# Seven-product f tiles from tile 1 on, first-half products first, and sums of h inside the norm chain

## The chip, the cores and the metric

The kernel runs on one core of a Trainium2 chip. The metric is the device time of one execution in microseconds. The engines are TensorE (PE, with its weight loads as PEld), VectorE (DVE), ScalarE (ACT), GpSimd (POOL) and SyncE (SP), which issues the transfers. Each engine works through its own queue in order and waits on semaphores for the others.

## The reference, cut to what matters

Two layers; each is a half-step SwiGLU feed-forward block, a token mixer (a 2-D Fourier transform in layer 0, neighbourhood attention in layer 1) and a second feed-forward block. Every one of these six sublayers has a norm ahead of it and one behind it, with scales and shifts that come from a modulation vector.

```python
def _modulation(cond, w_mod, b_mod):
    m = jax.nn.silu(cond) @ w_mod + b_mod
    return m.reshape(cond.shape[0], N_MOD, D_MODEL)

def _modulated_prenorm(x, g, m, k):
    return _rmsnorm(x, g) * (1 + m[:, 3 * k + 1, None]) + m[:, 3 * k, None]

def _swiglu(h, w1, w2):
    gate, up = jnp.split(h @ w1, 2, axis=-1)
    return (jax.nn.silu(gate) * up) @ w2

def _half_ffn(x, m, k, g_pre, g_post, w1, w2):
    h = _modulated_prenorm(x, g_pre, m, k)
    return x + 0.5 * m[:, 3 * k + 2, None] * _rmsnorm(_swiglu(h, w1, w2), g_post)
```

There are 640 tokens (512 latent, 128 context), D_MODEL is 1024 and D_FF 2816. All inputs are float32.

## The kernel before, in words

Data lies transposed: channels on the 128 partitions, tokens along the free dimension. A model width of 1024 is 8 chunks of 128, D_FF is 22 tiles of 128 ("f tiles"), and the 640 tokens are two halves of 320 columns. The sublayers are numbered n = 0 to 5; 0, 2, 3 and 5 are feed-forward, 1 is the Fourier mixer, 4 the attention.

**Precision.** Each operand is split in two parts, hi (ACT rounds it, L191 for weights and L202 for data) and lo (DVE subtracts hi, L193 and L203), and each product of a 128 x 128 weight block with 320 columns is three matmuls, hi by hi, hi by lo and lo by hi (`mm3`, L208 to L210). POOL takes the lo of six weight units at the start, DVE all others.

**Weights** arrive as units of 128 x 1024 (512 KB) in the pool `raw` of 4 buffers, and their hi and lo go to the pool `wts` of 6 pairs or, for some, to blocks of the ring of 20 blocks that also holds h, the hidden values and the stream x. `unit(i)` sends, that is loads and splits, up to three units ahead of the one that is asked for (`send`, L165).

**A feed-forward layer** (`ffn`, L514) multiplies h by w1 (gate and up, L517 on), applies silu(gate) * up, and multiplies the hidden tile by w2. Plain f tiles take 8 block products, each of 4 chunks by one half: gate and up, two halves of the chunks, two halves of the tokens. Fast f tiles (`w1_fast`, L586) take seven by a Strassen scheme: with gate and up as one factor, the first and second four chunks, and the two token halves, 2 x 2 blocks are multiplied with seven products of sums. For these, sums of the weights are formed on DVE as the unit is sent (L176 to L178, L184), sums of h are formed on DVE between the plain tiles of the second half (`combine`, L576, split at L203), and DVE adds the products up (L600 to L619). Before, tiles 4 to 19 are fast and 0 to 3, 20 and 21 plain. The plan (`plan_ffn`) runs tiles 0 and 1, 2, 3 for the first half of the tokens, the same for the second half with the steps of `combine` between them, then the fast tiles, and last 20 and 21. After tiles 4, 8, 12 and 16 it runs the w2 products of the slice before (8 output chunks by two halves), and at the end those of the last slice, one half after the other.

**Modulation.** The modulation vectors of later sublayers are formed beside the feed-forward layers: 128 products of a 128 x 1024 unit with the condition rows, two DVE instructions each (`gemv`, L348). BEHIND gives how many units a layer takes (28, 20, 28, 28, 24, 0); the calls of `w2` of the first four slices release them evenly (7 units a slice for 28). Their loads use the pool `raw` too.

**Norm chains.** At a layer's end and for each half a chain is launched (`boundary`): the post-norm of the layer, the addition to x, and the pre-norm of the next (`post`, `pre`). Its steps are woven into the stream of matmuls by a clock of estimated time (`tick`). Its two groups of small matmuls (L423 for the sums of squares, L431 to spread the result) are put behind the latest matmul in PE's queue at the place where the step runs. `pre` then scales y by the norm (L455), applies scale and shift (L461 on DVE for odd chunks, L463 on ACT for even), and splits the result into h (L202, L203). x is spilled to memory during the layer, to make room, and loaded back.

## Time and profile before

| what | value |
|---|---|
| time, median of 3 runs | 2402.0 us (2401.56 to 2404.12) |
| the profiled execution, its own time | 2403.8 us |
| its span, first to last instruction | 2402.0 us |
| mean granted clock of TensorE in it | 0.992 |
| PE busy | 2339.2 us, 15692 matmuls |
| DVE busy | 1740.3 us, 3112 instructions |
| ACT busy | 1275.4 us, 2436 instructions |
| DMA, read from memory | 263 MB, 114 GB/s over the span |

A row of the timeline has the start in us, the duration, the engine, the line of the code, the operation with what it writes and reads, the shape, a count of neighbours that were put together, and in brackets the idle time of the engine just ahead of it, with what ended it. A row of the groups has the busy time in us and the mean of one in ns, then the idle time ahead. Matmuls overlap, so their durations add up to more than the time they take.

### The profile page before, as it was taken

Reading aid. Unit: us, or ns where it says so; the run is one execution under the profiler, and the core shown is the slowest. Engines: PE = TensorE matmul, PEld = TensorE weight load, DVE = VectorE, ACT = ScalarE, POOL = GpSimd, SP = SyncE. Lnnn points to the kernel's source line nnn. Section 1 sums busy time; section 2 is a strip of 40 time slices with the busy share of each in tenths; the row PEclk is TensorE's granted clock in tenths of the full one; section 3 lists DMA queues with packets and bytes.
Section 4 is the critical chain, followed back from the end, with each engine's and each line's share of the span. In section 5 each row is a group of like instructions: output and inputs, shape, how many; then the busy total and the mean of one; then the engine's idle time right before and its main releaser. Section 6 shows DMA issues by size and latency. Waiting matters only on the chain.

```text
span 2402.0 us, 39473 instructions
## 1 busy us (share of the span) xinstructions
PE 2339.2 (97%) x15692; PEld 2264.2 (94%) x15692; DVE 1740.3 (72%) x3112; ACT 1275.4 (53%) x2436; POOL 48.3 (2%) x34
## 2 busy tenths in 40 slices
PE   6999999998999999999999999999999999999997
PEld 5899999998999999999999999997888899999997
DVE  7788878389788887838878885577777586665553
ACT  3445545564664554557445554745445574545545
POOL 3200000000000000000000000000000000000000
PEclk9899999999999999999999999999999999999998
DMA  7134344334523434443333444223333222322231
GB/s 260 58 124 149 119 132 136 116 100 132 158 90 120 143 114 132 132 132 106 113 123 109 139 150 158 71 77 118 123 113 124 66 102 71 97 78 64 88 133 44
DMA packets 80140, 277.09 MB, mean 115 GB/s; under 512 B 8786, under 2 KB 15186, under 8 KB 79956
## 3 DMA queue, kind: packets, MB, share of 16 engines
q1 hardware_dynamic: 79684, 274.25, 35.4%
q8 instruction: 123, 2.02, 0.3%
q14 instruction: 61, 0.50, 0.1%
q10 hardware_dynamic: 272, 0.33, 0.0%
HBM read 263.00 MB, written 11.53 MB: 114 GB/s over the span
## 4 chain that ended last, share of the span: by engine, by line
PE 88%; DVE 5%; ACT 3%; DMA 2%; issue 1%; POOL 0%; SPq 0%; ACTq 0%; DVEq 0%
PE main L208 25%; PE main L210 25%; PE main L209 25%; PE score L208 2%; PE score L209 2%; PE score L210 2%; PE sum L1065 2%; DVE junk L348 1%; PE turn L1052 1%; PE score L1039 1%; ACT hi L191 1%; DVE lo L193 1%; DVE ring L203 1%; PE sum L431 1%; PE sum L423 1%
## 5 line engine op out<-in xcount | busy, mean ns | idle before, releaser
L208 PE MATMUL main<-ring,hi 128*128 128x320 f32 x3872 | 1202.9, 312 | 19.4 <-ACT ring L202 18.1
L209 PE MATMUL main<-ring,hi 128*128 128x320 f32 x3872 | 1205.0, 311 | 1.6 <-DVE ring L203 1.5
L210 PE MATMUL main<-ring,lo 128*128 128x320 f32 x3872 | 1204.3, 311 | 2.3 <-POOL lo L193 2.3
L208 PEld LDWEIGHTS main<-ring,hi 128*128 128x128 f32 x3872 | 729.1, 189 | 28.6 <-ACT ring L202 20.5
L209 PEld LDWEIGHTS main<-ring,hi 128*128 128x128 f32 x3872 | 731.1, 189 | 7.0 <-DVE ring L203 3.6
L210 PEld LDWEIGHTS main<-ring,lo 128*128 128x128 f32 x3872 | 730.9, 189 | 5.8 <-POOL lo L193 2.8
L191 ACT ACTIVATE hi<-raw 128x1024 fp32r<-128x1024 f32 (+1 forms) x358 | 350.6, 982 | 476.1 <-PE main L209 382.3
L193 DVE TENSOR_TENSOR lo<-raw,hi 128x1024 fp32r<-128x1024 f32 (+1 forms) x354 | 398.1, 1125 | 163.7 <-ACT hi L191 162.9
L348 DVE SCALAR_TENSOR_TENSOR junk<-raw,wide 128x1024 bf16<-128x1024 f32 x256 | 312.8, 1222 | 16.8 <-DMA raw<-in_w_mod_t 14.4
L643 ACT ACTIVATE y<-main 128x320 f32<-128x320 f32 x320 | 137.9, 432 | 174.2 <-PE main L210 173.0
L384 DVE TENSOR_TENSOR total<-total,square 128x640 f32<-128x640 f32 x71 | 58.3, 823 | 115.8 <-ACT square L383 114.8
L631 ACT ACTIVATE main<-y 128x320 f32<-128x320 f32 x256 | 111.8, 439 | 23.5 <-DVE left L617 10.0
L209 PE MATMUL score<-ring,hi 128*128 128x320 f32 x384 | 118.7, 309 | 0.0
L208 PE MATMUL score<-ring,hi 128*128 128x320 f32 x384 | 118.7, 310 | 0.0
L210 PE MATMUL score<-ring,lo 128*128 128x320 f32 x384 | 118.6, 309 | 0.0
L193 DVE TENSOR_TENSOR lo<-sums,hi 128x1024 fp32r<-128x1024 f32 x64 | 78.2, 1222 | 52.5 <-ACT hi L191 52.5
L210 PE MATMUL main<-ring,ring 128*128 128x320 f32 x352 | 110.0, 313 | 5.8 <-POOL ring L193 5.8
L208 PE MATMUL main<-ring,ring 128*128 128x320 f32 x352 | 111.4, 317 | 0.0
L209 PE MATMUL main<-ring,ring 128*128 128x320 f32 x352 | 109.6, 312 | 0.0
L191 ACT ACTIVATE hi<-sums 128x1024 fp32r<-128x1024 f32 x64 | 67.9, 1061 | 28.0 <-PE main L209 20.5
L1054 ACT ACTIVATE right<-turn 128x384 f32<-128x384 f32 (+1 forms) x80 | 35.8, 448 | 84.5 <-PE turn L1052 84.3
L202 ACT ACTIVATE ring<-right 128x320 fp32r<-128x320 f32 x112 | 51.6, 468 | 46.2 <-DVE right L530 37.7
(195 smaller groups left out, 2820.6 us busy)
## 6 DMA issues: line engine op xcount, KB each, us to landing
raw<-in_w SPq DMA_DIRECT2D x264, 512.0 KB, 3.6
raw<-in_w_mod_t SPq DMA_DIRECT2D x128, 512.0 KB, 3.7
raw<-in_qkv SPq DMA_DIRECT2D x26, 512.0 KB, 3.6
spill<-ring SPq DMA_DIRECT2D x12, 640.0 KB, 3.4
ring<-spill SPq DMA_DIRECT2D x12, 640.0 KB, 4.8
raw<-in_bias SPq DMA_DIRECT2D x16, 448.0 KB, 3.3
first<-in_w_mod_t SPq DMA_DIRECT2D x8, 512.0 KB, 10.2
raw<-in_four_in SPq DMA_DIRECT2D x8, 512.0 KB, 3.6
```

The source lines that it names most:

```text
L191: nc.scalar.activation(hi, raw[:, at], AF.Copy)
L193: engine.tensor_tensor(lo, raw[:, at], hi.bitcast(F32), op=ALU.subtract)
L202: self.nc.scalar.activation(hi, src, AF.Copy)
L208: mm(out, whi, xhi, start=start, stop=False)
L209: mm(out, whi, xlo, start=False, stop=False)
L210: self.latest = mm(out, wlo, xhi, start=False, stop=stop)
L348: last = self.nc.vector.scalar_tensor_tensor(out=self.junk, in0=raw, scalar=1.0, in1=self.wide[:, cond, :], op0=ALU.mult, op1=ALU.mult, ac ...
L384: nc.vector.tensor_tensor(acc, acc, sq, op=ALU.add)
L631: nc.scalar.activation(ps[:, :HALF], self.y[:, m, lo:hi], AF.Copy)
L643: nc.scalar.activation(self.y[:, m, lo:hi], ps[:, :HALF], AF.Copy)
L1054: nc.scalar.activation(ptb[:, :w], pt[:, :w], AF.Copy)
L1065: nc.tensor.matmul(o, cache_v[:, ds] if k is None else v[:, k, ds], ptb[:, i * P + at : i * P + at + nq], start=n == 0, stop=n == len(tile ...
```

## The change

Tiles 1 to 21 are now fast and tile 0 is plain. To run before the second half of the tokens is ready, the gates of tiles 1 to 7 with the first half (`head`: two block products each, kept in a ring block) and all of tile 0's first half go first. `second` then takes tile 0's second half, its first four chunks as the first sum of h plus what the first half gave. `body(f)` runs a tile: tiles 1 to 7 have their gate products and take five more (their gate weights are loaded a second time, for the sum called mix), 8 to 19 take all seven, 20 and 21 take five and leave two, with mix, for `tail` behind the last w2 products of the first half. The sums of h move from the plan into `pre` of the second half (`combine(h, c)`), where they are formed chunk pair by chunk pair; chunks 0 to 3 of the second half are no longer split themselves. The writes of x to the spill move there too. The w2 slices are now of 2, 4, 5, 5 and 6 tiles instead of 4, 4, 4, 4 and 6, and run after tiles 2, 6, 11 and 16. The weight sums are written in another way, with as many additions per tile. A few lines have moved: L462 was L455 (scaling), L468 was L461, L491 was L576 (sums of h), L210 was L203 (lo of data), L200 was L193 (lo of weights), L182 and L186 were L176 to L184, L355 was L348, L215 to L217 were L208 to L210, L430 and L438 were L423 and L431.

```diff
-SLICES = ((0, 4), (4, 8), (8, 12), (12, 16), (16, 22))
-FAST = range(4, NF - 2)
+SLICES = ((0, 2), (2, 6), (6, 11), (11, 16), (16, 22))
+EARLY = ((1, 2), (3, 4), (5, 6, 7))
+LATE = (NF - 2, NF - 1)
...
+        elif (key, "sums") not in self.fast:
+            gate = self.raw_tile(srcs[0]) if len(srcs) > 1 else self.fast[key, "gate"]
+            up = self.raw_tile(srcs[-1])
+            sums = self.raw.tile([P, UNIT], F32, tag="raw", name=self.name("sums"))
+            add = lambda out, a, b: nc.vector.tensor_tensor(out, a, b, op=ALU.add)
+            add(sums[:, one], gate[:, one], up[:, one])
+            add(sums[:, two], sums[:, one], up[:, two])
+            add(gate[:, one], up[:, one], up[:, two])
+            nc.vector.scalar_tensor_tensor(out=gate[:, two], in0=gate[:, two], scalar=-1.0, in1=sums[:, two],
+                                           op0=ALU.mult, op1=ALU.subtract)
...
-            low = self.split(h.at(0, c, half, 2), h.at(1, c, half, 2), self.pair(self.y, c, half))
...
+            if h.quads and half:
+                if n:
...
+                    nc.sync.dma_start(out=self.spilled[c // 2], in_=self.xs[n][c // 2].rearrange("p c t -> p (c t)"))
+                self.combine(h, c)
+            else:
+                low = self.split(h.at(0, c, half, 2), h.at(1, c, half, 2), self.pair(self.y, c, half))
...
+            yield 2200 if c < 4 or not (h.quads and half) else 6000
+
+    def combine(self, h, c):
...
+        if c < 4:
+            h.steps[k] = [self.temp(kind).rearrange("p (c t) -> p c t", c=2) for kind in ("square", "total")]
+            put(1, h.steps[k][0], b12, b11)
+        else:
+            t1, t2 = h.steps[k]
+            put(2, t2, b22, t1)
+            put(3, t1, b22, b12)
+            put(4, t2, t2, b21)
+            self.split(h.at(0, c, 1, 2), h.at(1, c, 1, 2), b22)
...
+        def second():
+
+            parts = ("gate", "up")
+            pss = [self.bank()[:, :HALF] for _ in parts]
+            for i in range(2):
+                for kind, ps in zip(parts, pss):
+                    w = self.unit(base + self.w1_at[0, kind])
+                    for k in range(4):
+                        a = (4 * i + k) * P
+                        self.mm3(ps, w[0][:, a : a + P], w[1][:, a : a + P],
+                                 *(h.chunk(4 + k, 1) if i else h.sum(1, k)), i == k == 0, i == 1 and k == 3)
...
+        def body(f):
...
+            if ready:
+                c1, s = kept[f]
+                product(w, f, "mix", 0, lambda k: h.sum(1, k), True)
             else:
...
+                product(x, f, "gate", 0, lambda k: h.chunk(k, 0), True)
...
+            product(y, f, "sums", 512, lambda k: h.sum(2, k), True)
...
+            product(z, f, "sums", 0, lambda k: h.sum(3, k), True)
...
+            if not ready:
+                if not late:
+                    product(w, f, "mix", 0, lambda k: h.sum(1, k), True)
+                product(x, f, "gate", 512, lambda k: h.chunk(4 + k, 0), False)
...
+            product(z, f, "up", 0, lambda k: h.sum(4, k), False)
...
+        def rest(f, w, q, a):
+            product(w, f, "mix", 512, lambda k: h.chunk(4 + k, 1), False)
...
     def plan_ffn(self):
 
-        plan = []
+        plan = [("head", fs, None) for fs in EARLY]
+        due = 0
+        for f in range(NF):
+            plan.append(("body", f, None))
+            if f == SLICES[due][1]:
+                plan += [("w2", (due, m), half) for m in range(NCH) for half in (0, 1)]
+                due += 1
+        plan.append(("x", None, None))
         for half in (0, 1):
...
+            if half:
+                plan += [("tail", f, None) for f in LATE]
             plan += [("w2", (due, m), half) for m in range(NCH)]
```

The order of work at three places of n = 3. First PE's queue where the second half of the tokens comes in. Before (ring_11125 is h of the first half, ring_11435 and ring_11436 hi and lo of h of the second half, main_11455 tile 3 for the first half):

```order
L209 MATMUL main_11455<-ring_11126,ring_11319 128x320
L210 MATMUL main_11455<-ring_11125,ring_11320 128x320
L208 MATMUL main_11509<-ring_11435,hi_10714 128x320
L209 MATMUL main_11509<-ring_11436,hi_10714 128x320
L210 MATMUL main_11509<-ring_11435,lo_10715 128x320
L208 MATMUL main_11510<-ring_11435,hi_10747 128x320
```

After (ring_11223 is h of the first half, ring_11545 and ring_11546 hi and lo of the first sum of h, main_11498 and main_11499 gates of tiles 5 and 6 for the first half, main_11676 and main_11677 gate and up of tile 0 for the second):

```order
L216 MATMUL main_11498<-ring_11224,hi_11281 128x320
L217 MATMUL main_11498<-ring_11223,lo_11282 128x320
L215 MATMUL main_11676<-ring_11545,hi_10867 128x320
L215 MATMUL main_11677<-ring_11545,hi_10907 128x320
L215 MATMUL main_11499<-ring_11223,hi_11420 128x320
L216 MATMUL main_11499<-ring_11224,hi_11420 128x320
L217 MATMUL main_11499<-ring_11223,lo_11421 128x320
```

The first matmuls with the second half now read a sum of h, and its first two stand ahead of the last two gates of the first half.

Second, DVE's queue at the scaling of the second half in `pre`. Before (y is the normed value, square_11685 the first sum):

```order
L455 TENSOR_TENSOR y<-ring_10591,rms_11419 128x2x320
L203 TENSOR_TENSOR ring_11436<-y,ring_11435 128x640
L461 TENSOR_SCALAR y<-y,coef 128x192
L461 TENSOR_SCALAR y<-y,coef 128x128
L455 TENSOR_TENSOR y<-ring_10592,rms_11419 128x2x320
L576 TENSOR_TENSOR square_11685<-y 128x640
```

After (square_11542 and square_11580 are the first sum of h for chunks 0, 1 and for 2, 3; ring_11546 is its low part, lo_11551 the low part of tile 1's weight sums):

```order
L462 TENSOR_TENSOR y<-ring_10677,rms_11521 128x2x320
L462 TENSOR_TENSOR y<-ring_10678,rms_11521 128x2x320
L491 TENSOR_TENSOR square_11542<-y 128x640
L200 TENSOR_TENSOR lo_11551<-sums_11505,hi_11550 128x1024
L491 TENSOR_TENSOR square_11580<-y 128x640
L210 TENSOR_TENSOR ring_11546<-square_11542,ring_11545 128x640
L468 TENSOR_SCALAR y<-y,coef 128x192
```

The split of h's chunks 0 to 3 of the second half is gone from between the scalings, and the first sums of h with their split stand there instead.

Third, DVE's queue at the first modulation units, which the first w2 slice releases. Before, that slice runs after tile 4, whose last sums are left_11778 and right_11781; sums_12046 are the weight sums of tile 5, behind the slice, and lo_12051 their low part:

```order
L619 TENSOR_TENSOR left_11778<-left_11778,left_11779 128x320
L203 TENSOR_TENSOR ring_11777<-right_11781,ring_11777 128x320
L348 SCALAR_TENSOR_TENSOR junk,mod<-raw_12025,wide 128x1024
L203 TENSOR_TENSOR ring_11777<-left_11778,ring_11777 128x320
L176 TENSOR_TENSOR sums_12046<-raw_11974,raw_12044 128x512
L177 TENSOR_TENSOR raw_12044<-raw_12044 128x512
L178 TENSOR_TENSOR sums_12046<-raw_11974,raw_12044 128x512
L184 SCALAR_TENSOR_TENSOR raw_11974<-sums_12046,raw_11974 128x512
L348 SCALAR_TENSOR_TENSOR junk,mod<-raw_12081,wide 128x1024
L193 TENSOR_TENSOR lo_12051<-sums_12046,hi_12050 128x1024
```

After, the slice runs between tiles 2 and 3, and the piece is the end of seven modulation units: tile 4's weight sums are sums_12116, its mix is raw_12112 and the low part of that lo_12122; left_12110, left_12111 and right_12168 belong to tile 3, whose last product is main_12109:

```order
L355 SCALAR_TENSOR_TENSOR junk,mod<-raw_12102,wide 128x1024
L631 TENSOR_TENSOR right_12168<-left_12110,main_12108 128x320
L182 TENSOR_TENSOR sums_12116<-raw_12112,raw_12114 128x512
L642 SCALAR_TENSOR_TENSOR left_12110<-main_12109,left_12110 128x320
L632 TENSOR_TENSOR right_12168<-right_12168,ring_11247 128x320
L182 TENSOR_TENSOR sums_12116<-sums_12116,raw_12114 128x512
L644 TENSOR_TENSOR left_12111<-left_12111,left_12110 128x320
L210 TENSOR_TENSOR ring_12106<-right_12168,ring_12106 128x320
L182 TENSOR_TENSOR raw_12112<-raw_12114 128x512
L210 TENSOR_TENSOR ring_12106<-left_12111,ring_12106 128x320
L186 SCALAR_TENSOR_TENSOR raw_12112<-raw_12112,sums_12116 128x512
L200 TENSOR_TENSOR lo_12122<-raw_12112,hi_12121 128x1024
```

The next tile's weights still stand behind the last rows of the tile ahead of them, but between these two tiles PE's queue no longer has the w2 slice: tile 4 follows tile 3 at once. The modulation units (L355) stand ahead of both.

291 lines of the change are left out of this document (131 added, 160 removed).

## The prediction

> **What bounds the kernel now.** I read the page's summary and its chain of work that ended last, then the timeline of TensorE in a feed-forward layer, then the windows around the layers' starts and the timeline of VectorE there.
>
> ```profile
> PE 2339.2 (97%) x15692; PEld 2264.2 (94%) x15692; DVE 1740.3 (72%) x3112; ACT 1275.4 (53%) x2436; POOL 48.3 (2%) x34
> PE 88%; DVE 5%; ACT 3%; DMA 2%; issue 1%; POOL 0%; SPq 0%; ACTq 0%; DVEq 0%
> L208 PE MATMUL main<-ring,hi 128*128 128x320 f32 x3872 | 1202.9, 312 | 19.4 <-ACT ring L202 18.1
> 1093.83 0.31 PE L208 MATMUL main<-ring,hi 128*128 128x320 f32 x1
> ...
> 1097.94 0.31 PE L209 MATMUL main<-ring,hi 128*128 128x320 f32 x1
> ```
>
> On the average of the span TensorE (PE) is the bound: busy 97% of it, and 88% of the chain, while VectorE (DVE) works 72%. What one matmul is worth must not be taken from the group's mean of 312 ns, since matmuls overlap: from the first timeline row to the second are 28 matmuls, and (1097.94 − 1093.83) / 28 = 0.147 us each. The share of DVE is an average too, and the change works at one place. A layer's start looks different:
>
> ```profile
> 662.50:743.70 81.20, 81.20 (x560) 80.98 (x559) 69.54 (x112) 48.96 (x83) 0.00 (x0) 1.00 0.28 98
> 1108.45:1191.60 83.15, 83.15 (x560) 82.80 (x561) 72.08 (x115) 48.48 (x83) 0.00 (x0) 0.98 0.31 108
> 1135.35:1153.06 17.71, 17.71 (x123) 17.71 (x122) 17.71 (x30) 10.94 (x19) 0.00 (x0) 1.00 0.01 1
> ```
>
> These windows (length, then busy time and count of PE, of its weight loads, of DVE, ACT, POOL, then the clock) begin with the first matmul of the feed-forward layers n = 2 and n = 3 (of the sublayers 0 to 5; 0, 2, 3 and 5 are feed-forward). The first two hold about 540 product matmuls and the norms' small ones; call their starts T0. PE never waits after the first few us, but DVE is busy for 69.5 and 72.1 us of 81.2 and 83.2: its slack is a tenth here. In the third window, where the second half's norm and the sums of h run, DVE has none.
>
> **The change, term by term.** One: products. 16 tiles by 7 blocks and 6 by 8 are 160; 21 by 7 and one by 8 are 155. A block is 4 chunks by 3 matmuls, so 60 matmuls go per layer, 60 × 0.147 = **8.8 us**, four times 35.2 us (by the 312 ns it would be 75, which overlap already spends). PE's queue shows just these 240 fewer.
>
> Two: DVE. The moved work is not less, and each fast tile costs more of it than a plain one: five more tiles per layer form weight sums. What counts is what stands in DVE's queue ahead of the weights of a product on which PE waits. Pitches, start to start of neighbours in the timeline:
>
> ```profile
> 1130.18 1.22 DVE L193 TENSOR_TENSOR ring<-raw,ring 128x1024 fp32r<-128x1024 f32 x1
> 1131.32 0.49 DVE L413 TENSOR_TENSOR total<-total 128x320 f32<-128x320 f32 x1
> ...
> 1141.41 0.38 DVE L461 TENSOR_SCALAR y<-y,coef 128x192 f32<-128x192 f32 x1
> 1141.70 0.49 DVE L530 TENSOR_TENSOR right<-main,left 128x320 f32<-128x320 f32 x1
> 1142.10 0.82 DVE L203 TENSOR_TENSOR ring<-y,ring 128x640 fp32r<-128x640 f32 x1
> 1142.83 0.34 DVE L461 TENSOR_SCALAR y<-y,coef 128x128 f32<-128x128 f32 x1
> 1143.09 0.82 DVE L203 TENSOR_TENSOR ring<-y,ring 128x640 fp32r<-128x640 f32 x1
> ...
> 1151.58 0.82 DVE L576 TENSOR_TENSOR total<-y 128x640 f32<-128x640 f32 x1
> 1152.32 0.82 DVE L576 TENSOR_TENSOR total<-total,y 128x640 f32<-128x640 f32 x1
> ...
> 1197.24 0.69 DVE L193 TENSOR_TENSOR lo<-raw,hi 128x512 fp32r<-128x512 f32 x1
> 1197.85 1.22 DVE L348 SCALAR_TENSOR_TENSOR junk<-raw,wide 128x1024 bf16<-128x1024 f32 x1
> ...
> 1199.11 1.22 DVE L348 SCALAR_TENSOR_TENSOR junk<-raw,wide 128x1024 bf16<-128x1024 f32 x1
> 1200.26 0.08 DVE L348 DVE_READ_ACCUMULATOR junk<-raw,wide 128x1 f32 x1
> 1200.38 1.23 DVE L348 SCALAR_TENSOR_TENSOR junk<-raw,wide 128x1024 bf16<-128x1024 f32 x1
> ```
>
> So 1024 wide 1.14 us, 512 wide 0.60, 640 wide 0.735, 320 wide 0.40, the scale-and-shift of 192 and 128 columns 0.29 and 0.26, one modulation product 1.27. In the window of 17.71 us above, the rows summed with these pitches give 17.68.
>
> Three: the start of n = 3.
>
> ```profile
> 1108.45 0.85 PE L208 MATMUL main<-ring,hi 128*128 128x320 f32 x4 [2.24 <-ACT ring L202]
> ...
> 1110.19 0.47 PE L209 MATMUL main<-ring,hi 128*128 128x320 f32 x1
> 1110.46 0.47 PE L210 MATMUL main<-ring,lo 128*128 128x320 f32 x1
> 1135.35 1.56 DVE L455 TENSOR_TENSOR y<-ring,rms 128x640 f32<-128x640 f32 x2
> L191 ACT ACTIVATE hi<-sums 128x1024 fp32r<-128x1024 f32 x64 | 67.9, 1061 | 28.0 <-PE main L209 20.5
> ```
>
> Before, the second half's scaling (L455) begins at 1135.35, T0 + 26.9. Its small matmuls are pinned in PE's queue 147 product matmuls after the head's first, and 177 after the change: 30 × 0.147 = 4.4 us later, T0 + 31.3. From there DVE's queue of the changed kernel runs without a gap: to the last sum of h, 22 rows of 640, 8 scale rows, one of 1024, one of 512 = 16.2 + 2.2 + 1.1 + 0.6 = 20.1 us; then, to the low part of the mixed weights of tile 4, 14 rows of 512 (weight sums of tiles 2 to 4 and small splits), 31 of 320, 7 of 1024, 14 modulation products (released by the first w2 slice, which now comes after tile 2) and four tiny ones = 8.4 + 12.4 + 8.0 + 17.8 + 0.4 = 47.0 us. Ahead of the last row ScalarE rounds the same weights, 1.06 us, and hands them over: 1.2. So tile 4 can begin at 31.3 + 20.1 + 47.0 + 1.2 = T0 + 99.6. PE has only 216 + 48 + 3 × 60 + 96 = 540 matmuls ahead of it (head, second half of tile 0, tiles 1 to 3, first slice), which took 83.2 us before. It waits 16.4 us in all: some 6 to 9 of it at the second half of tile 0, for the sums and the second half of h, and the rest in front of tile 4. An idle PE is then slow: after the 2.24 us at 1108.45 matmuls start 0.27 apart for some 14 matmuls, 14 × (0.267 − 0.147) = 1.7 us, so I add 2. Sum: 16.4 + 2 − 8.8 = **+9.6 us**. The Trainium skill ("TensorE: Matmul & The Clock Gate", Part 1) has the clock fall only after an idle window of about 3.4 us; by that rule the 2.24 us would cost nothing more, and this trace differs, but the waits forecast here are longer than either.
>
> Four: n = 2, the same with its own rows.
>
> ```profile
> 688.28 1.56 DVE L455 TENSOR_TENSOR y<-ring,rms 128x640 f32<-128x640 f32 x2 [0.87 <-ACT rms L434]
> ...
> 1944.64 0.31 PE L208 MATMUL main<-ring,hi 128*128 128x320 f32 x1
> ...
> 1970.42 1.56 DVE L455 TENSOR_TENSOR y<-ring,rms 128x640 f32<-128x640 f32 x2 [0.86 <-ACT rms L434]
> ```
>
> The scaling began at T0 + 25.8 and is pinned 24 matmuls later: T0 + 29.3. DVE's queue to tile 4's weights holds 66.7 us, the wait 1.2: T0 + 97.2 against 81.2. 16.0 + 2 − 8.8 = **+9.2 us**.
>
> Five: n = 5 has no modulation products, and tile 4's weights stand far ahead in the queue. What is late is the second half of h for tile 0: T0 = 1944.64, scaling at T0 + 25.8 + 3.5 = 29.3, 19.4 us of rows, so T0 + 48.7; PE gets there after 268 matmuls and some 2 us of norm matmuls, 41.4. 7.3 − 8.8 = **−1.5 us**.
>
> Six: n = 0.
>
> ```profile
> 38.60:140.10 101.50, 90.21 (x553) 88.47 (x554) 82.82 (x124) 45.12 (x76) 21.81 (x6) 0.93 0.26 82
> 63.19 1.22 DVE L348 SCALAR_TENSOR_TENSOR junk<-first,wide 128x1024 bf16<-128x1024 f32 x1
> 80.35 6.99 POOL L193 TENSOR_TENSOR ring<-raw,ring 128x1024 fp32r<-128x1024 f32 x1 [11.78 <-ACT ring L191]
> 87.40 0.64 PE L210 MATMUL main<-ring,ring 128*128 128x320 f32 x1 [5.81 <-POOL ring L193]
> ```
>
> Here PE lost 20 us already (101.5 for matmuls worth 81), 5.8 of it behind POOL's split of a plain tile's weights, which goes. DVE's queue from the modulation product at 63.19 to tile 4's weights holds 77.1 us and, with the slow rows of the start, ends near 143, three us behind 140.1 where the 540 matmuls ended before. 3 + 2 − 8.8 = **−3.8 us**.
>
> Seven, what I cost at nothing. Tiles 8 to 19 have 84 matmuls, 12.3 us; DVE has 10.0 us of rows for each (5 of 512, 3 of 1024, 9 of 320 = 3.0 + 3.4 + 3.6), and the chain of one raw buffer (3.7 us of load, then the 8.1 us of these rows that stand between a tile's first sum and its last low part) is about 11.8. The 28 gates of tiles 1 to 7 that are loaded twice lie beside PE work. If that cover goes, it is a rival below. The spills only move.
>
> ```profile
> raw<-in_w SPq DMA_DIRECT2D x264, 512.0 KB, 3.6
> ```
>
> Sum: 9.6 + 9.2 − 1.5 − 3.8 = **+13.5 us**. The profiled execution took 2403.8 us (span 2402.0), so its like would take 2417.3; on the median of 2402.0 it is **2415.5**.
>
> **The rivals.**
>
> PE stays the bound: DVE is ready wherever PE comes. For it speak 97% against 72%. Against it stands the queue, whatever the durations: in n = 2 and 3 the rows for tile 4's weights stand behind the row that takes tile 3's last product. From PE's 540th matmul on come 5 rows of 320, 3 of 512, a rounding and a low part, 2.0 + 1.8 + 1.06 + 1.14 = 6.0 us with PE idle, then 2 us of slow clock. So the full 35.2 (2367) would need work between that PE does not have; with these two stalls alone the sum is 2 × (8.0 − 8.8) − 2 × 8.8 = −19, **2383**. The Trainium skill ("Perfetto Trace Analysis", Identifying the Most-Contended Engine) would have the engine of highest occupancy cut first, TensorE judged by its weight loads. These are at 94% here; by that rule the change cuts the right engine and this rival, up to 2367, would hold. The windows of the layers' starts speak against the average.
>
> Gain and loss cancel: DVE catches up on part, or the modulation products, whose place in time hangs on their loads, slip past. Half of the 16 us waits of n = 2 and 3 leaves 8 + 2 − 8.8 = +1 each: −3, **2399**.
>
> Slower still: four raw buffers pace the steady tiles. One tile needs three of them, its chain of 11.8 us has 0.5 us of slack against 12.3, and past that every us counts 12 × 4 times: a chain of 12.8 adds 0.5 × 48 = 24 us, **2439**; 13.3 gives 2463. For it: each load's 3.6 us is a median, and 28 loads are new; against it: ScalarE's rounding of weights waits mostly for PE now, that is, weights are loaded before they are wanted.
>
> ```profile
> ACT hi L191 <- PE main L209: 402.9, 218, 8.5
> ```
>
> That the change doesn't do what it says is excluded by the queue's 240 missing matmuls.
>
> **How the numbers follow.** Slower by DVE at the layers' starts, as summed: 0.5, own range 2407 to 2430 (2 us to either side per layer and the unknown slow clock). Cancelling, 2395 to 2407: 0.2. PE bound, 2367 to 2395: 0.2. Paced by buffers, above 2434: 0.1. A difference under 0.2%, 4.8 us, can't be told from none. Faster: 0.2 and a quarter of the cancelling case's 0.2 = 0.25; same: 0.15; slower: 0.6. The range 2380 to 2434 leaves out 0.1 above and some 0.08 below.
>
> **What would show it.** In n = 2 and n = 3 two gaps of PE in the first 100 us, of 4 to 9 us, ended by DVE or ACT rows of h's sums and of tile 4's weights, with DVE busy without a break ahead of them; DVE over 95% in that window; none at tile 4 of n = 5; the POOL stall of 5.8 us gone. A PE pitch of 0.147 and no gaps in tiles 8 to 19. I am wrong if PE's gaps at tile 4 are below 6 us, if DVE rows run at a shorter pitch than these, or if the steady tiles show gaps.

## The result and the profile after

| | before | after |
|---|---|---|
| median | 2402.05 us, 4 runs (2401.56 to 2404.12) | 2442.16 us, 4 runs (2440.63 to 2443.24) |
| ratio to before, 95% interval | | 1.0165 (1.0147 to 1.0182) |
| profiled execution, its own time and span | 2403.8, 2402.0 us | 2440.63, 2438.8 us |

The change makes the kernel 40 us slower. The forecast had the sign, but its 2415.5 us is 27 us short, and the result lies above the upper end of the range (2434). The page of the changed kernel, in its summary, its chain, its largest group and its weight loads:

```profile
PE 2323.6 (95%) x15452; PEld 2236.6 (92%) x15452; DVE 1859.0 (76%) x3316; ACT 1306.3 (54%) x2482; POOL 45.4 (2%) x34
PE 72%; DVE 14%; DMA 6%; ACT 5%; issue 3%; SPq 0%; DVEq 0%; ACTq 0%
L215 PE MATMUL main<-ring,hi 128*128 128x320 f32 x4032 | 1260.4, 314 | 68.8 <-ACT ring L209 32.8
raw<-in_w SPq DMA_DIRECT2D x292, 512.0 KB, 3.6
```

The 240 matmuls are gone (15452 for 15692), and the loads take 3.6 us as before. What changed is the chain: TensorE's share of it fell from 88% to 72%, VectorE's rose from 5% to 14%, and DVE works 119 us more (1859.0 against 1740.3).

Taken from each sublayer's first product matmul to the next one's, in the two traces:

| sublayer | before | after | difference | forecast |
|---|---|---|---|---|
| n = 0 | 465.2 | 472.4 | +7.2 | −3.8 |
| n = 1 | 158.6 | 155.9 | −2.7 | 0 |
| n = 2 | 446.0 | 460.9 | +14.9 | +9.2 |
| n = 3 | 448.0 | 462.7 | +14.7 | +9.6 |
| n = 4 | 388.2 | 389.3 | +1.1 | 0 |
| n = 5, to the end | 457.4 | 458.8 | +1.5 | −1.5 |

The differences add up to 36.7 us where the sum had 13.5, and nearly half of that miss of 23.2 us is in n = 0 (11.0 us). I start with n = 3, where the mechanism is plainest. First the timeline of DVE there, then that of PE (gaps and the matmuls at the slow pitch):

```profile
1159.18 1.56 DVE L462 TENSOR_TENSOR y<-ring,rms 128x640 f32<-128x640 f32 x2
...
1178.35 1.55 DVE L210 TENSOR_TENSOR ring<-y,ring 128x640 fp32r<-128x640 f32 x2
...
1217.84 1.22 DVE L355 SCALAR_TENSOR_TENSOR junk<-raw,wide 128x1024 bf16<-128x1024 f32 x1
1218.98 0.08 DVE L355 DVE_READ_ACCUMULATOR junk<-raw,wide 128x1 f32 x1
1218.98 0.48 DVE L618 TENSOR_TENSOR left<-left,main 128x320 f32<-128x320 f32 x1
1219.38 1.22 DVE L355 SCALAR_TENSOR_TENSOR junk<-raw,wide 128x1024 bf16<-128x1024 f32 x1
...
1226.56 0.69 DVE L186 SCALAR_TENSOR_TENSOR raw<-raw,sums 128x512 f32<-128x512 f32 x1
1228.37 1.23 DVE L200 TENSOR_TENSOR lo<-raw,hi 128x1024 fp32r<-128x1024 f32 x1 [1.12 <-ACT hi L198]
```

```profile
1127.99 1.44 PE L215 MATMUL main<-ring,hi 128*128 128x320 f32 x4 [2.50 <-ACT ring L209]
...
1165.15 0.62 PE L215 MATMUL main<-ring,hi 128*128 128x320 f32 x2 [4.28 <-ACT ring L209]
...
1166.73 0.47 PE L216 MATMUL main<-ring,hi 128*128 128x320 f32 x1
...
1172.06 0.44 PE L215 MATMUL main<-ring,hi 128*128 128x320 f32 x1
...
1185.80 0.42 PE L215 MATMUL main<-ring,hi 128*128 128x320 f32 x1 [0.97 <-DVE left L618]
...
1219.52 0.41 PE L215 MATMUL main<-ring,hi 128*128 128x320 f32 x1 [1.36 <-DVE left L618]
...
1228.39 0.64 PE L215 MATMUL main<-ring,hi 128*128 128x320 f32 x1 [5.08 <-ACT hi L198]
...
1237.26 0.39 PE L215 MATMUL main<-ring,hi 128*128 128x320 f32 x1 [0.67 <-DVE left L618]
...
1247.27 0.39 PE L215 MATMUL main<-ring,hi 128*128 128x320 f32 x1 [0.97 <-DVE left L618]
...
1295.71 0.41 PE L215 MATMUL main<-ring,hi 128*128 128x320 f32 x1 [1.22 <-DVE left L618]
```

With T0 = 1127.99 the scaling starts at T0 + 31.2 (forecast 31.3), and tile 4 at T0 + 100.4 (forecast 99.6). So the queue was counted rightly, and both forecast waits are there, though smaller than forecast: 4.28 us for 6 to 9 at the second half of tile 0, and 5.08 us at tile 4. Between them stand waits that end on L618 (0.97, 1.36 and one of 0.15 not shown), and waits go on behind tile 4. Most of them end on L618 too, the row that reads the bank of product z: PE may not add the next product (up) to that bank before it. DVE comes to it late, since modulation rows (L355) stand around it. The same stretch in windows (length, busy time and count of PE, its weight loads, DVE, ACT, POOL, then the clock):

```profile
1165.15:1185.80 20.65, 19.15 (x109) 18.57 (x109) 19.05 (x33) 10.88 (x21) 0.00 (x0) 0.83 0.09 25
1185.80:1219.52 33.72, 32.21 (x216) 31.68 (x216) 32.94 (x60) 15.51 (x30) 0.00 (x0) 1.00 0.58 187
...
1228.39:1247.27 18.88, 17.19 (x97) 16.32 (x97) 15.86 (x26) 5.66 (x9) 0.00 (x0) 0.86 0.38 112
1247.27:1295.71 48.44, 47.00 (x318) 46.47 (x318) 44.00 (x71) 27.84 (x52) 0.00 (x0) 1.00 0.54 175
1310.00:1537.12 227.12, 226.80 (x1548) 226.54 (x1546) 177.50 (x285) 113.25 (x193) 0.00 (x0) 1.00 0.40 121
```

Ahead of tile 4 DVE is busy for 32.94 of 33.72 us. Behind it, at 0.147 us a matmul, the 97 and 318 matmuls of the third and fourth rows are worth 14.3 and 46.7 us, so 4.6 and 1.7 us are lost there, 3.1 of it in the waits listed (0.67, 0.97, 1.22, and one of 0.23 not shown) and the rest at the lower clock. The last row is the steady tiles: 1548 matmuls in 227.12 us is 0.147 each. Nothing waits there, which excludes the rival of the four raw buffers for this layer.

In n = 0 (timelines of DVE, POOL and PE):

```profile
62.37 10.13 POOL L200 TENSOR_TENSOR lo<-raw,hi 128x1024 fp32r<-128x1024 f32 x3 [2.50 <-ACT hi L198]
...
63.42 2.35 DVE L368 TENSOR_TENSOR coef<-mod,vec 128x8 f32<-128x8 f32 x1
...
67.24 3.02 DVE L355 SCALAR_TENSOR_TENSOR junk<-ring,wide 128x1024 bf16<-128x1024 f32 x1
...
70.19 2.98 DVE L462 TENSOR_TENSOR y<-ring,rms 128x640 f32<-128x640 f32 x1
...
82.66 1.21 DVE L200 TENSOR_TENSOR lo<-raw,hi 128x1024 fp32r<-128x1024 f32 x1
...
83.93 0.63 PE L217 MATMUL main<-ring,lo 128*128 128x320 f32 x1 [8.28 <-DVE lo L200]
...
148.72 0.63 PE L215 MATMUL main<-ring,hi 128*128 128x320 f32 x1 [2.92 <-ACT hi L198]
```

The 5.81 us behind POOL is gone as forecast, but 8.28 us behind DVE stand in its place: the low part of the gate of tile 7, which `head` wants, lies in DVE's queue behind the second half's norm and first sums of h. Three of the rows ahead of it take 2.35 to 3.02 us while POOL runs (rows of these kinds take 0.15, 1.2 and 0.8 us elsewhere). Not every row is stretched: one of 128x1024 at 65.69 took 1.21 us in the same stretch.

### The profile page after: what moved, and what is told of

It is laid out like the page before. It is cut to its first block, busy times and chain, and to the rows that moved or that the text cites. A ratio compares the mean times of both kernels' runs of the same rounds, so it can differ in the third digit from the quotient of the medians.

```text
span 2438.8 us, 39344 instructions
## 1 busy us (share of the span) xinstructions
PE 2323.6 (95%) x15452; PEld 2236.6 (92%) x15452; DVE 1859.0 (76%) x3316; ACT 1306.3 (54%) x2482; POOL 45.4 (2%) x34
## 4 chain that ended last, share of the span: by engine, by line
PE 72%; DVE 14%; DMA 6%; ACT 5%; issue 3%; SPq 0%; DVEq 0%; ACTq 0%
PE main L215 21%; PE main L216 20%; PE main L217 20%; DMA raw<-in_w 4%; DVE junk L355 4%; DVE lo L200 3%; PE sum L1105 2%; ACT hi L198 2%; PE score L215 2%; PE score L216 2%; PE score L217 2%; DVE ring L210 1%; PE turn L1092 1%; PE score L1079 1%; DVE sums L182 1%
## 5 line engine op out<-in xcount | busy, mean ns | idle before, releaser
L215 PE MATMUL main<-ring,hi 128*128 128x320 f32 x4032 | 1260.4, 314 | 68.8 <-ACT ring L209 32.8
L217 PE MATMUL main<-ring,lo 128*128 128x320 f32 x4032 | 1254.8, 312 | 12.0 <-DVE lo L200 8.6
L216 PE MATMUL main<-ring,hi 128*128 128x320 f32 x4032 | 1257.5, 312 | 2.4 <-DVE ring L210 2.1
L215 PEld LDWEIGHTS main<-ring,hi 128*128 128x128 f32 x4032 | 762.3, 190 | 88.2 <-ACT ring L209 36.1
L217 PEld LDWEIGHTS main<-ring,lo 128*128 128x128 f32 x4032 | 763.1, 189 | 16.7 <-DVE lo L200 9.5
L216 PEld LDWEIGHTS main<-ring,hi 128*128 128x128 f32 x4032 | 763.9, 189 | 8.4 <-DVE ring L210 4.7
L200 DVE TENSOR_TENSOR lo<-raw,hi 128x1024 fp32r<-128x1024 f32 (+1 forms) x380 | 419.4, 1104 | 146.1 <-ACT hi L198 143.3
L355 DVE SCALAR_TENSOR_TENSOR junk<-raw,wide 128x1024 bf16<-128x1024 f32 x256 | 313.0, 1223 | 25.0 <-DMA raw<-in_w_mod_t 21.9
L200 DVE TENSOR_TENSOR lo<-sums,hi 128x1024 fp32r<-128x1024 f32 x84 | 102.5, 1221 | 37.5 <-ACT hi L198 37.4
L215 PE MATMUL score<-ring,hi 128*128 128x320 f32 x336 | 105.1, 313 | 0.1
L216 PE MATMUL score<-ring,hi 128*128 128x320 f32 x336 | 104.8, 312 | 0.0
L217 PE MATMUL score<-ring,lo 128*128 128x320 f32 x336 | 104.6, 311 | 0.0
L182 DVE TENSOR_TENSOR sums<-raw,raw 128x512 f32<-128x512 f32 x84 | 57.9, 690 | 37.3 <-DMA raw<-in_w 28.3
L618 DVE TENSOR_TENSOR left<-left,main 128x320 f32<-128x320 f32 x84 | 40.8, 485 | 34.8 <-PE main L217 34.0
L215 PEld LDWEIGHTS score<-ring,hi 128*128 128x128 f32 x336 | 64.1, 191 | 0.9 <-ACT hi L198 0.9
L216 PEld LDWEIGHTS score<-ring,hi 128*128 128x128 f32 x336 | 63.9, 190 | 0.0
## 6 DMA issues: line engine op xcount, KB each, us to landing
raw<-in_bias SPq DMA_DIRECT2D x16, 448.0 KB, 3.3
```

What stands on the lines that cost most here:

```text
L182: add = lambda out, a, b: nc.vector.tensor_tensor(out, a, b, op=ALU.add)
L200: engine.tensor_tensor(lo, raw[:, at], hi.bitcast(F32), op=ALU.subtract)
L215: mm(out, whi, xhi, start=start, stop=False)
L216: mm(out, whi, xlo, start=False, stop=False)
L217: self.latest = mm(out, wlo, xhi, start=False, stop=stop)
L355: last = self.nc.vector.scalar_tensor_tensor(out=self.junk, in0=raw, scalar=1.0, in1=self.wide[:, cond, :], op0=ALU.mult, op1=ALU.mult, ac ...
```

## The experiments

Each was timed beside the kernel before. "Change" is the changed kernel. Ratios are to before.

| label | median, us | runs | ratio (95%) |
|---|---|---|---|
| e1_mods_later | 2407.80 | 10 | 1.0019 (1.0010 to 1.0029) |
| e13_half_units | 2413.83 | 4 | 1.0051 (1.0037 to 1.0065) |
| e9_old_slices | 2411.85 | 4 | 1.0039 (1.0025 to 1.0053) |
| e15_before_later | 2403.36 | 11 | 1.0001 (0.9992 to 1.0010) |
| e2_mix_between | 2439.30 | 4 | 1.0149 (1.0132 to 1.0166) |
| e3_pool_one_more | 2442.64 | 4 | 1.0166 (1.0151 to 1.0182) |
| e4_more_gates | 2437.55 | 4 | 1.0146 (1.0131 to 1.0161) |
| e5_later_more_gates | 2409.25 | 7 | 1.0029 (1.0017 to 1.0040) |
| e14_no_pool | 2438.07 | 4 | 1.0145 (1.0131 to 1.0158) |
| e8_later_no_pool | 2400.89 | 10 | 0.9993 (0.9983 to 1.0002) |
| e6_later_copy_only | 2401.63 | 11 | 0.9994 (0.9986 to 1.0003) |
| e10_three | 2395.49 | 7 | 0.9973 (0.9962 to 0.9983) |
| e12_three_h_first | 2394.25 | 7 | 0.9968 (0.9957 to 0.9980) |
| e11_before_no_pool | 2391.27 | 5 | 0.9952 (0.9940 to 0.9964) |

### The modulation units ahead of tile 4

**e1** moves the seven units that the first w2 slice released to the three later slices; nothing else differs from the change.

```diff
-                    due = BEHIND[n] * passed // (2 * NCH * (len(SLICES) - 1))
+                    due = BEHIND[n] * max(passed - 2 * NCH, 0) // (2 * NCH * (len(SLICES) - 2))
```

> Only the place of the modulation units changes: the w2 slice after tile 2 releases none, the three later slices take all of them. Theory (VectorE's queue holds tile 4's weights behind 14 modulation products of 1.27 us): in n = 2 and 3 the wait of 5.1 us in front of tile 4, with its slow clock of some 3 us, falls under 2 us, in n = 0 that of 2.9 us too; 6 to 8 us less in n = 2 and 3 each and 3 to 5 in n = 0, so 2421 to 2427 us. Rival a (tile 4's weights are late for their loads or their raw buffers): the wait stays, 2438 to 2446. Rival b (VectorE is behind as a whole, and the units only move the wait): a new wait of the same size stands after tile 6 or 11, 2436 to 2446.

34 us come back, more than expected. PE's timeline in n = 3, and the waits for L618 of the whole run (total, times, longest), of the change first and of e1 second:

```profile
1146.90 0.58 PE L215 MATMUL main<-ring,hi 128*128 128x320 f32 x2 [4.28 <-ACT ring L209]
...
1167.55 0.41 PE L215 MATMUL main<-ring,hi 128*128 128x320 f32 x1 [0.97 <-DVE left L618]
...
1265.41 0.42 PE L215 MATMUL main<-ring,hi 128*128 128x320 f32 x1 [0.48 <-DVE left L618]
```

```profile
PE main L215 <- DVE left L618: 17.2, 17, 1.9
```

```profile
PE main L215 <- DVE left L618: 6.5, 7, 2.1
```

The wait at tile 4 is gone, and with it most waits for L618 behind it. n = 3 is 14.0 us shorter: 5.1 of the wait, 3.9 of L618 waits, and of the rest 3.2 are the slow matmuls behind tile 4 (6.3 us lost there less the 3.1 in waits).

**e13** lets the first slice release four of its seven units. It asks whether the time grows evenly with each unit or only past some number of them.

```diff
-                    due = BEHIND[n] * passed // (2 * NCH * (len(SLICES) - 1))
+                    due = BEHIND[n] * max(passed - NCH, passed // 2) // (2 * NCH * (len(SLICES) - 1) - NCH)
```

> The change, with the first w2 slice releasing 4 of the 7 modulation units (2 of 5 in the Fourier layer's neighbours counts as it falls out of the sum: 20 units give 2) and the others spread over the three later slices. Theory (VectorE's queue in front of tile 4 is too long by the wait there, its slow clock and the waits for L618, some 9 us in n = 2 and 3, and three units are 7.6 us): most of the gain of releasing none is there already, 2410 to 2420. Rival (each unit costs its 2.5 us from the first on): 3/7 of the 34 us, 2425 to 2430.

Three units fewer, 3 × 2 × 1.27 = 7.6 us of DVE rows per layer, bring 28 of the 34 us. At tile 4 of n = 3 PE waits 0.16 and 0.39 us where it waited 5.08:

```profile
1202.07 0.41 PE L215 MATMUL main<-ring,hi 128*128 128x320 f32 x1 [0.16 <-ACT hi L198]
...
1203.01 0.41 PE L215 MATMUL score<-ring,hi 128*128 128x320 f32 x1 [0.39 <-ACT hi L198]
```

So the cost doesn't grow evenly: the first four units cost 6 us and the last three 28. At which unit it turns was not measured.

**e9** takes the change with the old slices, so the first slice, and the units with it, stand behind tile 4 again.

```diff
-SLICES = ((0, 2), (2, 6), (6, 11), (11, 16), (16, 22))
+SLICES = ((0, 4), (4, 8), (8, 12), (12, 16), (16, 22))
```

> The change with its w2 slices put back (4, 4, 4, 4 and 6 tiles, run after tiles 4, 8, 12 and 16), so that the first modulation units come after tile 4 and beside 192 matmuls instead of 96. Theory (of the change's parts it is the early, short first slice that costs the time): the waits in front of tile 4 go in n = 0, 2 and 3, and 20 to 32 us of the 38 with them, 2410 to 2422. Rival (any place of the units in tiles 1 to 7 is as bad, since VectorE has no slack there): the waits move to tile 5 or 6, 2430 to 2444.

30 us come back by the slices alone. **e15** is the control: the units' move of e1, made in the kernel before.

```diff
-                    due = BEHIND[n] * passed // (2 * NCH * (len(SLICES) - 1))
+                    due = BEHIND[n] * max(passed - 2 * NCH, 0) // (2 * NCH * (len(SLICES) - 2))
```

> The kernel before with the modulation units of its first w2 slice moved to the later ones, as a control of the first experiment. Theory (in the kernel before VectorE has slack where its first slice stands, behind tile 4 and beside 192 matmuls): within 3 us of the kernel before. Rival (the later place is better in any kernel): 5 us or more below it.

Nothing moves. The units cost only where the change puts them.

### Is the wait for L618 a latency or lateness?

L618 reads z right before `up` is added to z, so a wait there might be only the turn-round of two engines. **e2** puts the product with mix between them for the tiles 1 to 7; the other tiles had it there already.

```diff
                 c1, s = kept[f]
-                product(w, f, "mix", 0, lambda k: h.sum(1, k), True)
...
                 tt(a, q, z, op=ALU.subtract)
+            if not late:
+                product(w, f, "mix", 0, lambda k: h.sum(1, k), True)
             if not ready:
-                if not late:
-                    product(w, f, "mix", 0, lambda k: h.sum(1, k), True)
```

> Only the order of products in tiles 1 to 7 changes: the first product with mix (12 matmuls, 1.8 us) runs between the two products that share bank z instead of first. Theory (in these tiles TensorE waits for L618 to read z before it may add to it, some 18 waits of 0.7 to 1.9 us in all, which I had not counted): the 17.2 us that matmuls idle for L618 fall under 5, and 12 to 20 us go, 2422 to 2430. Rival (VectorE is behind in tiles 1 to 4 anyway, so what these tiles gain is waited for in front of tile 4): only tiles 4 to 7 and n = 5 gain, 4 to 9 us, 2433 to 2438, and the waits in front of tile 4 of n = 2 and 3 grow by 2 to 4 us.

No gain clear of the noise (2.9 us, and the intervals overlap). The waits moved in front of tile 4, as this row of n = 3 shows (9.30 where the change had 5.08):

```profile
1233.93 0.64 PE L215 MATMUL score<-ring,hi 128*128 128x320 f32 x1 [9.30 <-ACT hi L198]
```

So they were DVE's lateness. Giving PE other work at one place only moves the wait to the next.

### The wait of n = 0 and the split on POOL

**e3** gives POOL one more unit, the late low part of tile 7's gate.

```diff
-        engine = nc.gpsimd if self.sent in range(2, 8) else nc.vector
+        engine = nc.gpsimd if self.sent in range(2, 9) else nc.vector
```

> Only the low part of the weights of the gate of tile 7 in n = 0 moves from VectorE to GpSimd. Theory (TensorE's wait of 8.3 us at 83.9 us in n = 0 is for this one row, which stands behind the second half's norm rows in VectorE's queue): the wait goes and n = 0 is 5 to 9 us shorter, 2433 to 2437. Rival (the second half's sums of h are as late, so TensorE waits at tile 0's second half instead; or GpSimd slows VectorE beside it): within 3 us of 2442.

No gain. The 8.28 us for `lo` became 10.08 us at a matmul that waits for ACT's eviction of the gates (L571):

```profile
89.56 0.63 PE L215 MATMUL main<-ring,hi 128*128 128x320 f32 x1 [10.08 <-ACT ring L571]
```

That eviction began only at 89.09 us. In ACT's queue it stands behind the roundings of the sums of h (L209), which from 80 to 87 us wait 0.54 to 0.81 us each for DVE's rows. So PE still waits for DVE's work on the second half, now by way of ACT.

**e8** is e1 with POOL taking none, and **e14** is the change with POOL taking none.

```diff
-        engine = nc.gpsimd if self.sent in range(2, 8) else nc.vector
+        engine = nc.gpsimd if self.sent in range(0) else nc.vector
```

> On top of the first experiment, GpSimd takes no low parts in n = 0, VectorE takes all. Theory (in n = 0 VectorE's rows stretch beside GpSimd: 2.35 us for 8 columns, 3.0 for a modulation product, 3.0 for 640, where 0.1, 1.27 and 0.74 stand elsewhere, and that makes the second half late there): six low parts cost VectorE 6.8 us and the stretching of 6 to 10 us goes, so n = 0 is the same or up to 5 us shorter, 2402 to 2409. Rival (GpSimd's share is what keeps VectorE up): n = 0 is 4 to 8 us longer, 2411 to 2416.

> The change with no low parts on GpSimd in n = 0, the modulation units where the change has them. Theory (11 of the 23 us by which the sum fell short lie in n = 0, and are the rows of VectorE that stretch beside GpSimd): n = 0 is 5 to 9 us shorter, 2433 to 2437. Rival (the modulation units bound n = 0's tile 4 anyway, and take back there what the head gains): 2438 to 2443.

e8 gains 6.9 us on e1, and its n = 0 is 7.9 us shorter, so giving DVE 6 more splits makes the start shorter. Whether that is the stretched rows or PE's own waits for POOL's splits (3.6 us in e1), which went too, these runs don't separate. In e14 the gain is 4.1 us, at the edge of the noise: tile 4 of n = 0 now waits 5.08 (it was 2.92), and the units take part of it back.

```profile
76.19 0.63 PE L217 MATMUL main<-ring,lo 128*128 128x320 f32 x1 [9.04 <-DVE lo L200]
...
144.01 0.63 PE L215 MATMUL main<-ring,hi 128*128 128x320 f32 x1 [5.08 <-ACT hi L198]
```

The first row shows that the wait for tile 7's gate isn't POOL's doing alone: it is 9.04 us with unstretched rows, only that it ends 7.7 us earlier in the span.

**e11** makes the same edit in the kernel before (its line names the same range).

> The kernel before, with no low parts on GpSimd in n = 0 and nothing else changed. Theory (GpSimd's split of 7 us for one unit and the stretched rows of VectorE beside it cost the kernel before too, as its 5.8 us wait behind GpSimd says): 4 to 9 us less, 2393 to 2399. Rival (what the edit gives is a matter of the changed head alone): 2401 to 2405.

2391.27 us, **the fastest kernel of all that ran**: POOL's share of the splits cost the kernel before 11.6 us, and n = 0 falls from 465.2 to 453.3. PE there waits 3.26 and 0.39 us where it waited 5.81, 2.16, 1.58 and 0.69.

### The first wait of a layer

**e4** puts the gates of tiles 8 and 9 in `head` too, so that PE has more to do until h of the second half comes; **e5** is the same on e1.

```diff
-EARLY = ((1, 2), (3, 4), (5, 6, 7))
+EARLY = ((1, 2), (3, 4), (5, 6, 7), (8, 9))
```

> Two more gates, of tiles 8 and 9, run on the first half of the tokens before the second half is needed: 48 matmuls, 7.0 us, for two more loads and two more low parts per layer. Theory (the 4.3 us wait at tile 0's second half, with 3 us of slow clock, is the price of sums of h that come right behind the norm): this wait goes in n = 2, 3 and 5, and the wait in front of tile 4 shrinks by what VectorE does in the 7 us; 5 to 8 us less in each of the three and 2 to 5 in n = 0, so 2414 to 2426. Rival (VectorE as a whole bounds tiles 0 to 4, and two more low parts cost it 2.3 us): n = 5 gains, n = 2 and 3 do not, 2433 to 2442.

> On top of the first experiment, two more gates (tiles 8 and 9) run on the first half of the tokens. Theory (tile 0's second half waits for a chain of fixed length): 7 us more of matmuls lie ahead of it, the 4.3 us wait goes, but the weights of the gates themselves come late by some 2.4 us as in the run before with more gates; 3 to 6 us less in n = 2, 3 and 5, 2390 to 2400. Rival (VectorE as a whole is the limit of tiles 0 to 4, two more low parts make it 2.3 us per layer): 2404 to 2412.

e4 gains some 5 us, at the edge of the noise, e5 nothing. In e4 the 4.28 us of n = 3 break up, and tile 4's wait stays:

```profile
1166.38 0.41 PE L215 MATMUL main<-ring,hi 128*128 128x320 f32 x1 [1.07 <-ACT hi L198]
...
1179.70 0.75 PE L215 MATMUL main<-ring,hi 128*128 128x320 f32 x2 [1.75 <-ACT ring L209]
...
1234.43 0.58 PE L215 MATMUL main<-ring,hi 128*128 128x320 f32 x1 [5.08 <-ACT hi L198]
```

**e6** looks at the chain ahead of that wait instead. ACT's timeline in n = 5 of the change has loads of its function table between the norm's steps, since `head` wants Silu (L571) while the norm wants Sqrt (L432):

```profile
2002.16 1.28 ACT L571 ACT_TABLE_LOAD   x1
...
2006.68 1.28 ACT L432 ACT_TABLE_LOAD   x1
...
2011.86 1.28 ACT L571 ACT_TABLE_LOAD   x1
```

e6 is e1 with Copy in `head` and the Silu in `body`.

```diff
-                        nc.scalar.activation(kept[f][kind == "up" or k == 7], ps, AF.Copy if k == 3 else AF.Silu)
+                        nc.scalar.activation(kept[f][kind == "up" or k == 7], ps, AF.Copy)
...
+                gate, s = s, self.temp("right")[:, :HALF]
+                with high():
+                    nc.scalar.activation(s, gate, AF.Silu)
```

> On top of the first experiment (modulation units later), the head's second gate half is taken from PSUM by a copy, and its silu is applied in the tile's body. Theory (what is left of the 4.3 us wait at tile 0's second half is ScalarE's: between the norm's small matmuls it loads its table for silu, for sqrt and for silu again, 3 x 1.28 us, and so the scaling comes late): the three table loads leave the chain in n = 2, 3 and 5, the wait falls from 4.3 to 1 to 2 us and with it the 3 us of slow clock, 4 to 6 us per layer, so 2390 to 2398. Rival (VectorE's rows behind the scaling, and not the chain, set the time, or the next wait is that of the sums): the wait stays or moves to the second half of h, 2403 to 2410.

6.2 us on e1, less than expected. The 4.28 us became 0.35 to 0.46 in n = 2, 3 and 5, but smaller waits follow in each, and in the two traces these layers are only 0.3, 2.0 and 2.1 us shorter; 3.9 us lie in n = 0, of which the theory had said nothing. This is n = 3 of e6 (L621 there is the change's L618):

```profile
1141.08 1.06 PE L215 MATMUL main<-ring,hi 128*128 128x320 f32 x3 [0.46 <-ACT ring L209]
...
1153.64 0.41 PE L216 MATMUL main<-ring,hi 128*128 128x320 f32 x1 [1.09 <-DVE ring L210]
...
1159.83 0.41 PE L215 MATMUL main<-ring,hi 128*128 128x320 f32 x1 [0.94 <-DVE left L621]
...
1164.92 0.41 PE L215 MATMUL main<-ring,hi 128*128 128x320 f32 x1 [1.31 <-ACT hi L198]
```

### All three together

**e10** joins the edits of e1, e6 and e8; **e12** adds that the split of the second half's h (chunks 4 to 7) goes ahead of the sums 2 to 4 in `combine`.

```diff
         else:
             t1, t2 = h.steps[k]
+            self.split(h.at(0, c, 1, 2), h.at(1, c, 1, 2), b22)
             put(2, t2, b22, t1)
...
-            self.split(h.at(0, c, 1, 2), h.at(1, c, 1, 2), b22)
```

> The three edits that paid, together: modulation units later, no silu in the head, no low parts on GpSimd in n = 0. Theory (three separate waits in separate places): the gains add, 2407.8 - 6.2 - 6.9 = 2394.7, so 2391 to 2398, below the kernel before. Rival (one wait hides another): 2398 to 2403.

> The three edits, and in the norm chain the second half's h (chunks 4 to 7) is split before the second to fourth sums of h. Theory (the 1.1 us wait that is left at tile 0's second half is for this split, last of the chain): it goes in n = 2, 3 and 5 and the sums come no later than tile 1 wants them, 2 to 5 us below the three edits alone. Rival (the sums that are put behind it are wanted at once by tile 1): no change within 2 us, or up to 4 us longer.

e10 comes to 2395.49, 7.4 us below the kernel before that was timed beside it: of the 13.1 us that the gains of 6.2 and 6.9 add up to, 12.3 are there. e12 is within 1.3 us of it, so the order in `combine` isn't what is left. With 240 fewer matmuls (35.2 us), e10 is still 4.2 us slower than e11, the like kernel without the change. By sublayer, from trace to trace, e10 is 4.6, 2.0 and 1.3 us longer than e11 in n = 0, 1 and 2, and 1.0, 0.8 and 0.5 us shorter in n = 3, 4 and 5. So the lag is mostly in n = 0, where PE's waits behind the first one add to 13.5 us up to 220 us of the span, against 4.6 in e11; 8.95 of the 13.5 are the wait for tile 7's gate. In the other layers the saving is about eaten up. How, in n = 3 of e10 (windows, from T0 on):

```profile
1101.94:1190.00 88.06, 83.27 (x548) 81.02 (x549) 76.63 (x119) 57.91 (x105) 0.00 (x0) 0.98 0.35 114
1134.33:1160.00 25.67, 21.62 (x136) 20.30 (x137) 25.14 (x43) 17.61 (x31) 0.00 (x0) 0.98 0.09 29
```

548 matmuls are worth 80.4 us and took 88.1: 7.7 us are lost, of the 8.8 that a layer saves; before lost 1.0 us in 560. In the second row, where PE's remaining waits lie, DVE is busy for 25.14 of 25.67 us. These rows show DVE full there; no run took rows out of that stretch alone, so that its work is the whole of the residue in these layers is argued, not shown. Nor did any run bring tile 7's gate forward in DVE's queue in n = 0.

## Why the prediction was right and wrong

**What bounds.** Right: the layers' starts decide, not the averages. PE stays the most occupied engine (95%, its weight loads 92%) while 240 of its matmuls less make the kernel slower, so the rival that PE is the bound falls. With it falls, in this case, the reading by the Trainium skill ("Perfetto Trace Analysis", Identifying the Most-Contended Engine) that the engine of highest occupancy should be cut first.

**Terms one and two.** Right: 240 matmuls at 0.147 us, and the DVE pitches.

**Three and four, n = 3 and n = 2.** The mechanism is shown by e1, e13 and e9, with e15 as control: modulation products in DVE's queue ahead of tile 4's weights. The time of tile 4 was forecast within 0.8 us in n = 3, and within 1.5 in n = 2 (T0 + 98.7 for 97.2). What failed is the term **"+ 2"** for all that comes behind tile 4. I took DVE to have caught up once tile 4's weights were there. It had not: in n = 3, 4.6 + 1.7 = 6.3 us were lost behind tile 4, in further waits for L618 and at the slow pitch. With tile 4's 0.8, less the 2 that I had added, that is the 5.1 us by which n = 3 is over. e2 shows that those waits are the same lateness, and e1 that they go with it. In n = 2 it is 6.2 us behind tile 4 (98.7 − 81.2 = 17.5 at tile 4, and 14.9 + 8.8 − 17.5), and in n = 0 it is 7.5 (below). So the term was 6 us over the three layers and the runs showed 20.0: 14.0 of the 23.2 us. Of the rest, 7.8 lie in the time of tile 4 (5.5 of them in n = 0), 3.0 in n = 5, and −1.6 in n = 1 and 4.

The gaps themselves were cut otherwise than forecast. The prediction called itself wrong if PE's gaps at tile 4 were below 6 us, and they were 5.08 (n = 2 and 3) and 2.92 (n = 0). DVE was as late as I had summed, but in n = 3 PE spent 2.5 us of it waiting for L618 ahead of tile 4, and some 3 on slow matmuls behind the first gap (109 matmuls worth 16.0 us in the window of 20.65, 1.5 of it waits). DVE's queue sets the time of tile 4, however PE's idle time ahead of it is divided, and only the division was wrong.

**Five, n = 5.** −1.5 forecast, +1.5 measured. The wait of 7.3 us was looked for at the second half of h at T0 + 48.7. It came earlier, at T0 + 36.4, since the first two matmuls with the first sum of h stand in PE's queue ahead of two gates (as the order of the change showed), and 0.97 followed at L618. This is the timeline of PE there, and the window between its two rows:

```profile
2016.41 0.90 PE L215 MATMUL main<-ring,hi 128*128 128x320 f32 x2 [4.28 <-ACT ring L209]
...
2036.44 0.42 PE L215 MATMUL main<-ring,hi 128*128 128x320 f32 x1 [0.97 <-DVE left L618]
...
2016.41:2036.44 20.03, 18.82 (x108) 18.15 (x108) 19.04 (x33) 10.86 (x21) 0.00 (x0) 0.85 0.09 27
```

PE's waits come to 6.2 us (4.28, 0.97, and 0.70 and 0.24 not shown), less than the 7.3. What the sum left out is the slow matmuls: the 108 of the window are worth 15.9 us and took 20.03, 1.2 of it waits, so 2.9 us went to the lower clock. Here the sum had no "+ 2".

No gap at tile 4 of n = 5: right, since this layer has no modulation units. Part of the 4.28 us hung on ACT's table loads, which the sum did not have (e6).

**Six, n = 0.** The worst step, −3.8 for +7.2. Half of it is the time of tile 4: it began at 148.72 us, T0 + 109.9, where I had DVE's queue end near 143, so 8.5 us later than before and not 3. The other half is "+ 2" again, for 7.5. I summed DVE's rows to tile 4 with little allowance for the start and took the POOL stall as a gain. PE's waits behind the first one add to 24.5 us up to 220 us of the span, against 11.2 before: 13.3 more, less 8.8 of matmuls is +4.5, and the remaining 2.7 is nearly all slow pitch behind the waits. Up to 220 us the change ran 990 matmuls, worth 145.5 us, in 181.2, and the kernel before ran 1098, worth 161.4, in 181.3. So the change lost 15.8 us more, and 13.3 of them are the waits. Of the 13.3, 2.5 is the swap of 5.81 us for 8.28. I had not looked at what stands in DVE's queue ahead of the gate of tile 7, which the change makes PE want early.

**Seven.** The steady tiles cost nothing, as forecast, and no wait of TensorE behind the start is put down to a load. n = 1 gained 2.7 and n = 4 lost 1.1 us where 0 was forecast; I found no cause for these. Among the 16 traces n = 1 takes 155.9 to 159.9 us and n = 4 386.7 to 389.3, though no experiment's edit is in them, so differences of this size stand between like traces too.

**The range** reached to 2434 because the only case above it was that of the buffers (0.1). The case that came, the same mechanism at 2.7 times the size (36.7 us between the two traces for 13.5), was given 2 us to either side per layer, with no row behind that bound. The bound should have come from DVE's slack in the tiles behind tile 4.

## What to carry to other kernels

Where a change trades work of one engine for work of another, count the second engine's queue from the place where the work comes in until it has caught up, not to the first wait only; each later hand-over in that stretch may wait again. Background work that is released by a count of progress moves when the progress is re-cut: look at what it now stands ahead of (here 34 of 40 us). And try a part of the kernel that both versions share by itself; here it gave the fastest version, from the kernel before.

## What the runs showed of the hardware

A wait of 4.28 us leaves PE slow for longer than I took from the 2.24 us case: behind 1165.15 the matmuls from 1166.73 to 1172.06 start 0.267 us apart (20 steps; behind the 2.24 us of the kernel before it is 12, from 1109.93 to 1113.13), and the windows with waits have clocks of 0.83 to 0.86.

Some of DVE's rows stretch beside POOL's tensor-tensor, small ones far more than in proportion: 128 x 8 took 2.35 us beside it, 0.15 elsewhere. With no splits on POOL (e14) rows of 128 x 8, 128 x 1024 and 128 x 640 in the same place took 0.17, 1.22 and 0.83 us, where 2.35, 3.02 and 2.98 had stood. Six fewer units on POOL and six more on DVE made n = 0 of the kernel before 11.9 us shorter.
